# HGRN2, DeltaNet and S5 layer: three pieces of head 0's projections traced between S5's input groups

## The chip, the core and the metric

The kernel runs on one core of one Trainium2 chip. The metric is the device time of one execution in microseconds (us), the median over several executions.

The names of the engines: PE multiplies matrices, DVE, ACT and POOL work element by element (POOL the slowest, DVE and POOL on tensors, ACT with functions), and SP issues all DMAs here. Each engine takes its instructions from a row of its own, in the order of the row.

## What is computed

One layer of a backbone with three token mixers over 512 latent tokens and a prefix of 256 context tokens, of width 1024, in float32. After an RMSNorm and a modulation, one projection gives the inputs of all three: HGRN2 (four heads, both directions), a gated DeltaNet (four heads) and S5, a complex diagonal state space over 32 groups of 16 channels with 64 states. The three are mixed by gates; a residual add and an MLP follow. Of the reference, what this case touches is the preparation of HGRN2 and the scan of S5:

```python
qh = _heads(silu(q), A_HEADS);  vh = _heads(i, A_HEADS)
fval = lbb + (1.0 - lbb) * sigmoid(z)          # z: a forget gate per direction
args = [(qh, _heads(1.0 - fval[d], A_HEADS), vh, _heads(log(fval[d]), A_HEADS)) for d in range(2)]
...
def _s5_scan(u, ar, ai, bbr, bbi, x0r, x0i):
    """x_n = Lbar x_{n-1} + Bbar u_n from x0. u (B,N,G,16); returns state re/im (B,N,G,S)."""
```

The modulation comes from a product of the conditioning vector with a matrix `ada_w` of 1024 columns for each of its parts.

## The kernel before

The kernel is one program without loops on the chip: Python writes out every instruction, and a list scheduler then orders each engine's row. It goes by the order in which the instructions were traced, and pulls an instruction ahead where those before it in the trace must wait. All DMAs are issued by SP (L62), so they stand in one row too. Tiles come from pools, and a tile can be written only when the one that had its place is no longer read: `s4` (512 KB) has 8 places, `s2` 12, `nt` (1 MB) 2, `raw` 3, `hi` and `lo` 2 each, and in PSUM `pj` has 3, `tr` and `mm` 2 each, `att` 1.

`project` makes one block of 128 columns of the projection. Its weights are loaded (`raw`, 512 KB, L62), split into a rounded part on ACT (`hi`, L224) and the rest on DVE (`lo`, L225), and multiplied in three products (L245 to L247): 24 matmuls of 128x512 for the latent tokens, and 24 of 128x256 for the context where it is wanted.

The stretch in question follows the norm of the input. Its parts:

- S5's input u: four blocks of the projection (`U_C`, L1248 to L1254), each stored by two DMAs into `s5du` and `s5dul`.
- `state_in` (L347 to L374) makes S5's inputs, in eight groups of four channel groups. Each multiplies B by powers of the poles (`spread`, L337 to L346; groups 0, 1, 4, 5 and 6 on POOL, 2, 3 and 7 on DVE), transposes the result on PE (L364), copies it on ACT (L366), multiplies it by U on PE (L369; U is loaded for each second group) and copies that into `sv` (L371 to L373). Then `scan` (L376 to L385) steps through 94 tokens on POOL.
- `ada_gates` (L1228) sums three products of `ada_w` with the conditioning vector: 12 loads of 1 MB into `nt`, for each two sums on DVE (L1200; the first of each product on ACT, L1198), then sums over partitions on PE (L1211) and a small addition on DVE (L1212). One step of it is traced with each group of `state_in`, the last part (`last_sums`) later.
- `hgrn2_in` (L1264 to L1295) makes one head's inputs in five pieces: two gates F (`project`, tanh on ACT L1272, scaling on DVE L1273), the values V (with transposes on PE, L1282), then Q and G (ACT L1244, DVE L1245).
- `taps` (L417 to L447) makes S5's output filter, in eight groups as well: S5's C is loaded into an `nt` place, DVE prepares it (L425, two copies L431 and L432 for every second group) and multiplies it by powers of the poles (L408 to L410), PE transposes (L438 to L441), ACT copies (L443), and two DMAs store it (`s5dk`). Its DVE work is held behind what was traced for DVE before it (`queued`).
- Head 0's chunks then begin with cumulative sums on DVE (L514 to L518), transposes (L523), an ACT copy (L525), and products (L530, L552).

`mix` takes one piece of each of its generators in turn. Before, `hgrn2_in(0)`, `taps` and `last_sums` are mixed after all of S5's inputs.

Of the kernel before, what the change touches and what calls it, by code (L numbers as in the profile page):

```python
# [1031 lines left out]
def hybrid_block(ctx, tc, x, cc, xc, ada_w, columns, w_in, a_log, dt_bias, lam, s5_b, s5_c, w_glu, w_ba, w_bb, w_bc,  # L1032
# [18 lines left out]
    s5 = S5(k)  # L1051
# [113 lines left out]
    def project(col, lat=True, con=True, m=128, first=False):  # L1165

        wh, wl = W.load(w_in, col, 8, m)
        res = []
        for on, n, xh, xl in ((lat, 512, hh, hl), (con, 256, ch, cl)):
            if not on:  # L1170
                continue
            p = k.p("pj", [m, n])
            if first:
                for kt in range(8):
                    nc.tensor.matmul(p, wh[:, kt], xh[:, kt], start=kt == 0, stop=False)
                    nc.tensor.matmul(p, wl[:, kt], xh[:, kt], start=False, stop=False)
                for kt in range(8):
                    nc.tensor.matmul(p, wh[:, kt], xl[:, kt], start=False, stop=kt == 7)
            else:
                for kt in range(8):  # L1180
                    mm3(nc, p, wh[:, kt], wl[:, kt], xh[:, kt], xl[:, kt], kt == 0, kt == 7)
            res.append(p)
        return res if len(res) > 1 else res[0]
# [4 lines left out]
    def ada_rest(j, acc, fetch, engine):  # L1188

        kt = 0  # L1190
        while kt < 8:
            two = fetch()
            n = two.shape[1]
            k.dma(two, ada_w[128 * kt:128 * (kt + n), 1024 * j:1024 * j + 1024].rearrange("(x p) m -> p x m", p=128))
            for i in range(n):
                w, c = two[:, i], cs[:, kt + i, 0:1]
                if not kt + i:
                    nc.scalar.activation(acc, w, AF.Copy, scale=c)  # L1198
                elif engine is v:
                    v.scalar_tensor_tensor(acc, w, c, acc, op0=OP.mult, op1=OP.add)  # L1200
                else:
                    nc.scalar.activation(w, w, AF.Copy, scale=c)
                    engine.tensor_tensor(acc, acc, w, op=OP.add)
            kt += n
            if kt % 2 == 0:
                yield
        yield
        m = mod2[:, j - 2]
        p = k.p("att", [128, 8])
        for b in range(8):  # L1210
            nc.tensor.matmul(p[:, b:b + 1], acc[:, 128 * b:128 * b + 128], k.one, start=True, stop=True)  # L1211
        v.tensor_tensor(m, p, at["ada_b"][:, 8 * j:8 * j + 8], op=OP.add)  # L1212
        if j == 4:
            v.scalar_tensor_tensor(m, m, 1.0, at["n2"], op0=OP.add, op1=OP.mult)
            v.tensor_scalar(m, m, -1.0 / 256, None, op0=OP.mult)
        if j in (2, 5):
            if j == 2:
                v.tensor_scalar(m, m, 0.5, None, op0=OP.mult)
            p = k.p("att", [8, 128])
            nc.tensor.transpose(p, m, k.ident)  # L1220
            r = consts.tile([8, 128], FT, name=f"r{j}")
            nc.scalar.activation(r, p, AF.Copy)
            k.dma(drow[j // 3].rearrange("(b n) -> b n", b=8), r)
        yield

    def ada_gates():

        done = iter(())  # L1228
        for j in (2, 3, 4):
            g = ada_rest(j, k.t("s4", [128, 1024]), lambda: k.t("nt", [128, 2, 1024]), v)  # L1230
            for i in range(4):
                next(g)

                if i == 1:
                    for _ in done:
                        pass
                yield
            done = g
        yield done

    def silu2(out, p, x=None):

        t = k.t("pst", [128, p.shape[-1]])
        nc.scalar.activation(t, p, AF.Tanh, scale=0.5)  # L1244
        v.scalar_tensor_tensor(out, t, 1.0, p, op0=OP.add, op1=OP.mult)  # L1245


    for b in range(4):  # L1248
# [3 lines left out]
        nc.scalar.activation(u[:, :, 0:32], pc.rearrange("p (w r) -> p r w", r=8), AF.Copy)  # L1252
        k.dma(s5.du[b].rearrange("c g x -> g c x"), u.rearrange("p a b -> p (a b)"))
        k.dma(s5.dul[128 * b:128 * b + 128].rearrange("p (r w) -> p r w", r=8), u[:, :, 32:96])  # L1254
    ada = ada_gates()
    for _ in s5.state_in():
        next(ada)
    s5.scan()
    for last_sums in ada:
        pass  # L1260


    dn = {n: [k.d(f"n{n}{h}", [128, 512]) for h in range(4)] for n in "abc"}

    def hgrn2_in(h):

        F, FC = k.t("s4", [128, 2, 512]), k.t("s2", [128, 2, 256])
        for d in range(2):
            pl, pc = project(F_A + 512 * (1 - d) + 128 * h)
            z = 4 * d + h  # L1270
            for o, p in ((F[:, d], pl), (FC[:, d], pc)):
                nc.scalar.activation(o, p, AF.Tanh, scale=0.5)  # L1272
                v.tensor_scalar(o, o, lb[:, 1, z:z + 1], lb[:, 2, z:z + 1], op0=OP.mult, op1=OP.add)  # L1273
            yield
        V = k.t("s4", [128, 6, 128])
        pl, pc = project(V_A + 128 * h)
        for p, n, c0 in ((pc, 2, 0), (pl, 4, 2)):
            y = k.t("pst", [128, n, 128])
            nc.scalar.activation(y.rearrange("p a b -> p (a b)"), p, AF.Copy)
            pt = k.p("tr", [128, n, 128])  # L1280
            for t in range(n):
                nc.tensor.transpose(pt[:, t], y[:, t], k.ident)  # L1282
            nc.scalar.activation(V[:, c0:c0 + n], pt, AF.Copy)
        yield
        q = k.t("s2", [128, 512])
        silu2(q, project(Q_A + 128 * h, con=False))
        yield
        g = k.t("s2", [128, 512])
        silu2(g, project(G_A + 128 * h, con=False))
        heads[h] = HG(k, q, F, FC, V), g  # L1290
        yield
# [93 lines left out]
    def gate(n, b, to=None):  # L1385
        g = k.t("fg", [128, 512])
        nc.scalar.activation(g, project(GATES + 1024 * n + 128 * b, con=False), AF.Tanh, scale=0.5)
        if to is None:
            k.dma(dg[n][b], g)
        return g  # L1390

    def gates(n, blocks):
        for b in blocks:
            gate(n, b)
            yield
# [57 lines left out]
    def mix(*gs):  # L1453

        gs = list(gs)
        while gs:
            for g in list(gs):
                try:
                    yield next(g)
                except StopIteration:  # L1460
                    gs.remove(g)
# [12 lines left out]

    save = lambda to: lambda b, g: k.dma(to[b], g)
    s4 = lambda: k.t("s4", [128, 1024])
    taps = s5.taps()
    for _ in chain(mix(hgrn2_in(0), taps, last_sums), gates(0, range(0, 1))):
        pass
    weave(hgrn2(0), chain(hgrn2_in(1), context(0), gates(0, range(1, 2))), (3, 1), (4, 2), (1, 2), (8, 0), (2, 1))  # L1480
    weave(hgrn2(1), chain(hgrn2_in(2), mix(context(1), scalars_in())), (2, 1), (4, 1), (1, 1), (3, 2), (8, 3))
# [44 lines left out]
    for b, _ in enumerate(branch("b", w_bb, range(8), prev=mg[1], last=merged)):  # L1526
        wo += resident(w_out, 128 * b, 1, lambda shape: k.t("xn", shape), nc.gpsimd)
        if b >= 4:
            i = b - 4
# [297 lines left out]
```

## Time and profile before

| | |
|---|---|
| median of three executions | 1385.56 us (1382.54 to 1385.8) |
| profiled execution | 1387.55 us |
| its span, first to last instruction | 1385.8 us |
| mean granted clock of PE | 0.956 |
| PE busy | 1268.2 us (92%) |
| DVE, ACT, POOL busy | 957.0 (69%), 481.4 (35%), 338.7 us (24%) |
| DMA | 167.59 MB, 54.4% of 16 engines' time |

Busy times are of one execution. The granted clock is a share of 2.4 GHz, and at any moment it is 1 or 0.5. A row of the timeline has the start of an instruction, its time, the engine, the line of the kernel, the operation with its result and operands, and in brackets how long the engine had been idle before it and what ended that. Matmuls overlap, so the distance of two starts counts, not the time of one. In the table by stage the columns behind the stretch and its length are the busy times of PE, of PE's weight loads, of DVE, ACT and POOL (in brackets the number of instructions), then PE's granted clock, the mean share of the 16 DMA engines and the rate. The trace writes `s` for tiles of several pools and `in_s_c` for S5's C.

### The profile page before, as it was taken

Reading aid. Unit: us, or ns where it says so; the run is one execution under the profiler, and the core shown is the slowest. Engines: PE = TensorE matmul, PEld = TensorE weight load, DVE = VectorE, ACT = ScalarE, POOL = GpSimd, SP = SyncE. Lnnn points to the kernel's source line nnn. Section 1 sums busy time; section 2 is a strip of 40 time slices with the busy share of each in tenths; the row PEclk is TensorE's granted clock in tenths of the full one; section 3 lists DMA queues with packets and bytes.
Section 4 is the critical chain, followed back from the end, with each engine's and each line's share of the span. In section 5 each row is a group of like instructions: output and inputs, shape, how many; then the busy total and the mean of one; then the engine's idle time right before and its main releaser. Section 6 shows DMA issues by size and latency. Waiting matters only on the chain.

```text
span 1385.8 us, 18357 instructions
## 1 busy us (share of the span) xinstructions
PE 1268.2 (92%) x6781; PEld 1039.0 (75%) x6781; DVE 957.0 (69%) x1794; ACT 481.4 (35%) x889; POOL 338.7 (24%) x483
## 2 busy tenths in 40 slices
PE   7888899999999878899988899969979999999996
PEld 2477767888778777689876888847878878788885
DVE  6937677895777946988756975546657699674336
ACT  3425322433333435532233022233344345434222
POOL 0337599999400860000000000023000000000002
PEclk9889899999999989999998899979989999999998
DMA  9776752455856667581374345688405455633231
GB/s 360 139 129 213 180 74 42 62 107 43 82 78 114 87 86 192 111 94 23 72 123 151 84 87 108 133 194 268 123 16 182 137 154 155 178 95 103 91 107 61
DMA packets 184378, 167.59 MB, mean 121 GB/s; under 512 B 24865, under 2 KB 152545, under 8 KB 184289
## 3 DMA queue, kind: packets, MB, share of 16 engines
q1 hardware_dynamic: 184288, 166.43, 54.4%
q8 instruction: 53, 0.87, 0.3%
q14 instruction: 37, 0.30, 0.1%
HBM read 147.53 MB, written 18.87 MB: 120 GB/s over the span
## 4 chain that ended last, share of the span: by engine, by line
PE 63%; DVE 17%; DMA 13%; issue 4%; ACT 3%; SPq 1%; POOL 0%; POOLq 0%; DVEq 0%; ACTq 0%
PE pj L245 13%; PE pj L247 13%; PE pj L246 13%; DVE lo L225 3%; PE mm L887 3%; PE mm L878 2%; PE att L552 2%; DMA nt<-in_ada_w 2%; PE pj L1622 2%; DMA raw<-in_w_in 2%; DVE s L1200 1%; DMA xn<-in_w_out 1%; DMA s<-s5du 1%; DMA fg<-na 1%; PE mm L1622 1%
## 5 line engine op out<-in xcount | busy, mean ns | idle before, releaser
L225 DVE TENSOR_TENSOR lo<-raw,hi 128x1024 fp32r<-128x1024 f32 (+1 forms) x171 | 201.4, 1182 | 162.5 <-ACT hi L224 159.3
L224 ACT ACTIVATE hi<-raw 128x1024 fp32r<-128x1024 f32 (+1 forms) x171 | 164.6, 964 | 384.1 <-PE pj L246 241.9
L245 PE MATMUL pj<-hh,hi 128*128 128x512 f32 (+1 forms) x512 | 211.7, 413 | 4.9 <-ACT hi L224 4.5
L246 PE MATMUL pj<-hl,hi 128*128 128x512 f32 (+1 forms) x512 | 208.8, 408 | 0.0
L247 PE MATMUL pj<-hh,lo 128*128 128x512 f32 (+1 forms) x512 | 208.4, 407 | 0.0
L246 PE MATMUL pj<-hc,hi 128*128 128x512 f32 (+1 forms) x528 | 187.5, 355 | 0.0
L247 PE MATMUL pj<-h,lo 128*128 128x512 f32 (+1 forms) x304 | 116.9, 385 | 2.6 <-DVE lo L225 2.6
L245 PE MATMUL pj<-h,hi 128*128 128x512 f32 (+1 forms) x304 | 116.8, 385 | 2.5 <-ACT h L237 1.6
L245 PEld LDWEIGHTS pj<-hh,hi 128*128 128x128 f32 (+1 forms) x512 | 99.3, 194 | 23.9 <-ACT hi L224 5.0
L247 PEld LDWEIGHTS pj<-hh,lo 128*128 128x128 f32 (+1 forms) x512 | 98.5, 192 | 19.8 <-DVE lo L225 0.6
L246 PEld LDWEIGHTS pj<-hc,hi 128*128 128x128 f32 x528 | 102.7, 195 | 12.8 <-DVE hc L238 0.2
L246 PEld LDWEIGHTS pj<-hl,hi 128*128 128x128 f32 (+1 forms) x512 | 98.5, 192 | 17.3 <-issue 0.2
L245 PE MATMUL pj<-hc,hi 128*128 128x256 f32 (+2 forms) x256 | 84.9, 332 | 19.0 <-ACT hi L224 10.0
L247 PE MATMUL pj<-hc,lo 128*128 128x256 f32 (+2 forms) x256 | 84.5, 330 | 4.4 <-DVE lo L225 4.4
L1004 POOL TENSOR_SCALAR_AFFINE_SELECT s<-s 128x512 f32<-128x512 f32 x8 | 5.8, 753 | 301.3 <-DVE s L832 89.5
L1770 POOL TENSOR_TENSOR xn<-x,row 128x512 f32<-128x512 f32 x8 | 10.3, 1282 | 276.4 <-DVE x L1543 273.8
L247 PEld LDWEIGHTS pj<-h,lo 128*128 128x128 f32 x304 | 58.6, 193 | 14.5 <-DVE lo L225 3.8
L245 PEld LDWEIGHTS pj<-h,hi 128*128 128x128 f32 x304 | 58.7, 194 | 14.2 <-ACT h L237 2.0
L245 PEld LDWEIGHTS pj<-hc,hi 128*128 128x128 f32 (+1 forms) x256 | 50.6, 198 | 23.4 <-ACT hi L224 11.3
L247 PEld LDWEIGHTS pj<-hc,lo 128*128 128x128 f32 (+1 forms) x256 | 50.6, 197 | 8.5 <-DVE lo L225 5.9
L382 POOL TENSOR_TENSOR sw<-sp,sv 128x64 f32<-128x64 f32 x94 | 50.3, 535 | 20.6 <-ACT sv L372 13.4
L383 POOL TENSOR_TENSOR sw<-sp,sv 128x64 f32<-128x64 f32 x94 | 53.9, 574 | 0.0
(618 smaller groups left out, 2750.1 us busy)
## 6 DMA issues: line engine op xcount, KB each, us to landing
raw<-in_w_in SPq DMA_DIRECT2D x72, 512.0 KB
raw<-in_w_ff SPq DMA_DIRECT2D x66, 512.0 KB
nt<-in_ada_w SPq DMA_DIRECT2D x12, 1024.0 KB
aw<-in_ada_w SPq DMA_DIRECT2D x8, 512.0 KB
dg<-fg SPq DMA_DIRECT2D x16, 256.0 KB
fg<-dg SPq DMA_DIRECT2D x16, 256.0 KB
mg<-fg SPq DMA_DIRECT2D x16, 256.0 KB
fg<-mg SPq DMA_DIRECT2D x16, 256.0 KB
```

Of the source, the lines that this page charges most:

```text
L224: K.nc.scalar.activation(hi, w, AF.Copy)
L225: (engine or K.nc.vector).tensor_tensor(lo, w, hi.bitcast(FT), op=OP.subtract)
L245: nc.tensor.matmul(out, wh, xh, start=start, stop=False)
L246: nc.tensor.matmul(out, wh, xl, start=False, stop=False)
L247: nc.tensor.matmul(out, wl, xh, start=False, stop=stop)
L382: e.tensor_tensor(t[:, 1], aa[:, 1], ap(x, 96 * G, [[-96 * G, 2], [96, G]]), op=OP.mult)
L383: e.tensor_tensor(t[:, 0], aa[:, 0], x, op=OP.mult)
L552: nc.tensor.matmul(pa[:, c], kd[:, 128 * c:128 * c + 128], rhs, start=True, stop=True)
L878: nc.tensor.matmul(pq[:, u], M[:, u], ap(X, 128 * u, [[2 * m, 64 // m], [n + m, 2], [1, m]]), start=True, stop=True)
L887: nc.tensor.matmul(py[:, u], zt[:, u], q[:, u], start=True, stop=True)
L1200: v.scalar_tensor_tensor(acc, w, c, acc, op0=OP.mult, op1=OP.add)
L1622: nc.tensor.matmul(p[i], a[l][:, j, 128 * i:128 * i + 128], x[:, c], start=first and x is wh and not l, stop=last and x is wl)
```

## The change

The block that traces `ada_gates`, `state_in` and `scan` moves down, behind the definitions that `hgrn2_in` needs, and three pieces of `hgrn2_in(0)` are now drawn inside of it: both F after groups 1 and 3 and V after group 5. Q and G stay with the taps.

```diff
-    ada = ada_gates()
-    for _ in s5.state_in():
-        next(ada)
-    s5.scan()
-    for last_sums in ada:
-        pass
...
     s4 = lambda: k.t("s4", [128, 1024])
+    ada, into = ada_gates(), hgrn2_in(0)
+    for i, _ in enumerate(s5.state_in()):
+        next(ada)
+        if i in (1, 3, 5):
+            next(into, None)
+    s5.scan()
+    for last_sums in ada:
+        pass
+
     taps = s5.taps()
-    for _ in chain(mix(hgrn2_in(0), taps, last_sums), gates(0, range(0, 1))):
+    for _ in chain(mix(into, taps, last_sums), gates(0, range(0, 1))):
         pass
```

The lines of `hgrn2_in` are lower by 7 after the change (L1272 and L1273 become L1265 and L1266). The instructions are the same ones; the rows of PE, DVE, ACT, POOL and SP differ from S5's inputs to the end of the taps, and read alike again from L530 on.

SP at the last stores of u and the first ada loads, before (`nt` are ada loads, `raw` weights of the projection, `s<-s5du` U):

```order
L62 DMA raw_1987<-in_w_in 128x8x128
L62 DMA s_92_827<-s5du_561 128x8x96
L62 DMA s5dul<-s_90_820 1024x1x64
L62 DMA s_112_914<-s5du_562 128x8x96
L62 DMA s5du_564<-s_90_820 8x16x768
L62 DMA nt_954<-in_ada_w 128x2x1024
L62 DMA nt_996<-in_ada_w 128x2x1024
```

and after:

```order
L62 DMA raw_1936<-in_w_in 128x8x128
L62 DMA s_92_883<-s5du_561 128x8x96
L62 DMA s5dul<-s_90_820 1024x1x64
L62 DMA nt_1072<-in_ada_w 128x2x1024
L62 DMA s5du_564<-s_90_820 8x16x768
L62 DMA nt_1114<-in_ada_w 128x2x1024
L62 DMA nt_1219<-in_ada_w 128x2x1024
L62 DMA s_118_1032<-s5du_562 128x8x96
```

An ada load took the place of the second U, which stands behind three of them now.

SP up to the load of C (`nt<-in_s_c`), before:

```order
L62 DMA nt_1143<-in_ada_w 128x2x1024
L62 DMA nt_1185<-in_ada_w 128x2x1024
L62 DMA raw_2029<-in_w_in 128x8x128
L62 DMA raw_2259<-in_w_in 128x8x128
L62 DMA nt_1660<-in_ada_w 128x2x1024
L62 DMA nt_1664<-in_ada_w 128x2x1024
L62 DMA nt_1678<-in_ada_w 128x2x1024
L62 DMA nt_1682<-in_ada_w 128x2x1024
L62 DMA raw_2315<-in_w_in 128x8x128
L62 DMA nt_1804<-in_s_c 128x1024
```

and after:

```order
L62 DMA raw_2315<-in_w_in 128x8x128
L62 DMA drow<-r_1278 8x128
L62 DMA nt_1909<-in_ada_w 128x2x1024
L62 DMA nt_1913<-in_ada_w 128x2x1024
L62 DMA s_172_1352<-s5du_564 128x8x96
L62 DMA raw_2402<-in_w_in 128x8x128
L62 DMA nt_1927<-in_ada_w 128x2x1024
L62 DMA nt_1931<-in_ada_w 128x2x1024
L62 DMA raw_2487<-in_w_in 128x8x128
L62 DMA nt_1970<-in_s_c 128x1024
```

The two `raw` that stood together ahead of the last four ada loads are further up, and others stand singly between these loads.

DVE from C's first operation (L425) on, before:

```order
L425 TENSOR_SCALAR nt_1804<-nt_1804 128x512
L408 TENSOR_TENSOR nt_1805<-nt_1804,sp_422 128x512
L409 TENSOR_TENSOR s_284_1875<-nt_1804,sp_422 128x512
L408 TENSOR_TENSOR nt_1805<-nt_1804,sp_422 128x512
L410 TENSOR_TENSOR nt_1805<-nt_1805,s_284_1875 128x512
L1212 TENSOR_TENSOR mod_579<-att_1882,cols 128x8
L409 TENSOR_TENSOR s_284_1875<-nt_1804,sp_422 128x512
L1214 SCALAR_TENSOR_TENSOR mod_579<-mod_579,cols 128x8
L225 TENSOR_TENSOR lo_2262<-raw_2259,hi_2261 128x1024
```

and after:

```order
L425 TENSOR_SCALAR nt_1970<-nt_1970 128x512
L1212 TENSOR_TENSOR mod_579<-att_2023,cols 128x8
L225 TENSOR_TENSOR lo_2318<-raw_2315,hi_2317 128x1024
L1245 SCALAR_TENSOR_TENSOR s_298_1979<-pst_2011,pj_1986 128x512
L431 COPY nt_1970<-sp_422 64x16x16
L432 COPY nt_1970<-sp_422 64x16x16
L408 TENSOR_TENSOR nt_1971<-nt_1970,sp_422 128x512
L409 TENSOR_TENSOR s_303_2016<-nt_1970,sp_422 128x512
L408 TENSOR_TENSOR nt_1971<-nt_1970,sp_422 128x512
L410 TENSOR_TENSOR nt_1971<-nt_1971,s_303_2016 128x512
```

L1212, an L225, an L1245 and the copies L431 and L432 (which stood ahead of L425) are now between L425 and the first tap operations, L408 to L410.

## Rows read from the trace of the kernel before

**Rows 1.** Stages: us, each engine's busy us, granted clock, DMA share, GB/s.

```profile
92.80:175.00 82.20, 67.39 (x412) 58.42 (x411) 56.54 (x54) 35.71 (x80) 49.13 (x51) 0.88 0.70 186
175.00:240.70 65.70, 64.36 (x434) 45.78 (x433) 52.36 (x75) 13.31 (x20) 61.62 (x106) 0.99 0.40 57
240.70:352.00 111.30, 108.91 (x696) 93.93 (x696) 81.35 (x144) 41.53 (x77) 102.76 (x219) 1.00 0.54 72
174.99:233.65 58.66, 57.74 (x391) 41.23 (x391) 48.77 (x70) 12.10 (x17) 55.21 (x91) 0.99 0.39 54
178.58:240.30 61.72, 61.27 (x423) 43.66 (x423) 48.78 (x69) 11.37 (x17) 57.80 (x100) 1.00 0.39 57
```

**Rows 2.** PE's waits from 92 to 242 us: total, times, longest.

```profile
PE mm L369 <- DMA s<-s5du: 5.9, 1, 5.9
PE tr L364 <- POOL s L346: 3.6, 2, 2.8
PE mm L369 <- ACT s L366: 1.6, 2, 0.8
```

**Rows 3.** Table by stage, two shorter stretches.

```profile
137.00:146.00 9.00, 6.14 (x29) 5.60 (x30) 7.84 (x7) 2.34 (x6) 3.53 (x3) 0.62 1.04 212
151.66:155.60 3.94, 3.94 (x21) 3.94 (x22) 0.41 (x1) 1.25 (x4) 1.40 (x5) 0.58 0.38 148
```

**Rows 4.** Chain that ended last, in order of time: start, us, what.

```profile
97.87 1.14 SPq L62
...
101.22 8.73 DMA nt<-in_ada_w
...
139.60 16.19 DMA nt<-in_ada_w
...
166.25 8.71 DMA nt<-in_s_c
...
240.08 0.61 ACT s L525
...
353.17 13.77 DMA raw<-in_w_in
```

**Rows 5.** Timeline of DVE: start, us, operation, idle before and its releaser.

```profile
174.99 0.43 DVE L425 TENSOR_SCALAR nt<-nt 128x512 f32<-128x512 f32 x1 [3.05 <-DMA nt<-in_s_c]
...
233.65 0.85 DVE L514 TENSOR_TENSOR_SCAN s<-s,one 128x256 f32<-128x256 f32 x1
...
236.00 0.57 DVE L518 TENSOR_TENSOR s<-s,s 128x255 f32<-128x255 f32 x1
```

**Rows 6.** Timeline of PE.

```profile
176.99 0.39 PE L246 MATMUL pj<-hl,hi 128*128 128x512 f32 x1
177.22 0.40 PE L247 MATMUL pj<-hh,lo 128*128 128x512 f32 x1
...
178.58 0.39 PE L438 MATMUL tr<-nt,nt 128*48 128x128 f32 x2 [0.50 <-DVE mod L1212]
...
240.73 1.16 PE L530 MATMUL mm<-s,s 128*128 128x128 f32 x8 [0.45 <-ACT s L525]
```

**Rows 7.** DVE's groups from 174.9 to 233.7: busy us, mean ns, idle before.

```profile
L408 DVE TENSOR_TENSOR nt<-nt,sp 128x512 f32<-128x512 f32 x16 | 12.7, 824 | 0.0
...
L225 DVE TENSOR_TENSOR lo<-raw,hi 128x1024 fp32r<-128x1024 f32 x5 | 6.4, 1281 | 3.5 <-ACT hi L224 3.5
...
L1245 DVE SCALAR_TENSOR_TENSOR s<-pst,pj 128x512 f32<-128x512 f32 x2 | 1.4, 676 | 0.0
...
L431 DVE COPY nt<-sp 64x256 f32<-64x256 f32 x3 | 0.9, 291 | 4.7 <-PE tr L441 4.7
...
L1212 DVE TENSOR_TENSOR mod<-att,cols 128x8 f32<-128x8 f32 x1 | 0.2, 154 | 0.0
```

**Rows 8.** Timeline of POOL.

```profile
154.05 0.35 POOL L382 TENSOR_TENSOR sw<-sp,sv 128x64 f32<-128x64 f32 x1 [13.36 <-ACT sv L372]
...
451.28 1.50 POOL L456 TENSOR_SCALAR sp<-sp 128x512 f32<-128x512 f32 x1 [88.20 <-DMA sp<-in_s_c]
```


## Prediction

> **What bounds the kernel now.** I read the table of stages first [rows 1]. From 92.8 us (S5's first transposes) to 175 (the taps begin) PE works only 67.39 of 82.2 us, at a mean granted clock of 0.88; from 175 on it is full: 64.36 of 65.7, then 108.91 of 111.3. So time can be won where it waits or runs at its lower clock, and that is in the first of these stages. Their waits (82.2 - 67.39, and 65.7 - 64.36) are 16.15 us. The list of PE's waits [rows 2] says for what: 5.9 for the load of the first U, most of the rest for POOL's spreads and for ACT's copies of S5's transposes. The windows around 140 and 153 [rows 3] show the other loss: behind such waits PE's clock falls to 1.2 GHz, and its mean is 0.62 and 0.58 there.
>
> PE does not set the beginning of the taps, though. That is done by a chain through SP and DVE: loads of ada weights, with legs of 8.73 and 16.19 us, DVE's sums on them, and then the load of S5's C with 8.71 us [rows 4], after which DVE's first tap work, L425, starts at 174.99 [rows 5]. From the first tap transpose at 178.58 [rows 6] PE is the late one: there DVE idles 4.7 us for PE's transposes (L431) and 3.5 us for ACT's `hi` (L225) [rows 7].
>
> **The change part by part.** No operation is added or removed; some are moved.
>
> *Projections that go ahead of the taps.* By the printed order, PE has 101 matmuls of 128x512 and 72 of 128x256 between S5's first transposes and the first tap transpose before, and 147 and 72 now: 46 of 128x512 leave the taps stage. Two of them start 0.23 us apart at full clock [rows 6], so 46 x 0.23 = 10.6 us of PE work. The stage from the first L438 to the last matmul ahead of L530 holds 61.27 us of PE work now [rows 1], then 50.7.
>
> *Where they go.* Into PE's waits between 108 and 178. The 5.9 us for U stand ahead of all moved work and stay; of the 16.15 at most 10.3 can be filled, which is the limit of the gain at an unchanged clock. The fill should also keep the clock up where it fell: 6.14 x (1 - 0.62) + 3.94 x (1 - 0.58) = 4.0 us [rows 3].
>
> *When the taps can begin.* DVE's ada sums stay as they are. In SP's new order an ada load stands ahead of U1's load and S5's last store, at the place that SP reaches at 97.87 instead of 101.22 [rows 4]: 3.3 us early. Against it, DVE's row now mixes these sums with an L225 and an L1266 that wait for the moved projection, and has group 2's spread behind four more sums than before. I take L425 at 173.8, 1.2 us earlier. Bounds: 171.6 (all of the 3.3 kept) and 188.8 (the third rival). Behind L425 stand now, ahead of the four operations that make the first tap tile (0.8 us each), one L225 (1.28), one L1245 (0.68), two copies (0.3 each) and an addition of 0.2 (L1212) [rows 7]: with L425's 0.43, 6.4 us, so the first L438 is at 180.2, 1.6 us later than before.
>
> *The end of the stage.* By PE: 180.2 + 50.7 = 230.9, and L530 0.4 behind, as from 240.30 to 240.73 now [rows 1, 6]: 231.3. By DVE: from L425 to L514 it took 58.66 us [rows 5]; out of it go the 4.7 of waits for PE and 2.0 for an L225 and an L1245 that fall away behind L438, and 0.7 for two copies comes in: 52.7, so L514 at 226.5. Four more small DVE operations follow to 236.57 now [rows 5], 2.9 us; then four L523 and ACT's L525, which I estimate at 1.5 us together from the 0.61 of L525 [rows 4] and four transposes: L530 at 230.9. The two chains end within half a microsecond of each other and hand tiles to each other eight times; a wait of PE for ACT in S5's groups, the nearest such hand-over, is 0.8 us (1.6 in 2) [rows 2]. None would make it 231.3, one at each group 237.7; I take two or three, 2 us, since the transposes of a group have projections between them on PE. L530 moves from 240.73 to 233.2: **7.5 us**.
>
> *What is delayed.* S5's inputs. Until the last L369 PE now has 57 more matmuls of 128x512 and 48 more of half that: 57 x 0.23 + 48 x 0.12 = 18.9 us, of which some 9 fall into its waits. And POOL's row brings a spread of group 5 second, which needs a slot that group 2's transposes free, so POOL stands from about 110 to 124. The scan then starts near 164 instead of 154.05 [rows 8]. It costs nothing: behind the scan POOL waits 88.2 us for a load [rows 8], and nobody waits for the scan. Without that cover the price would be the 10 us.
>
> *Behind L530* every engine's order is the same in both, and PE is full to 352 [rows 1], so what is won is carried on. The next place that could swallow it is the weight load at 353.17, 13.77 us on the chain [rows 4]. It is issued when a buffer is free, behind the projections of that stage, so I let it move with them.
>
> The profiled execution took 1387.55 us (span 1385.8 and 1.75 around it), 2 above the median of 1385.56. Its sum is 1387.55 - 7.5 = 1380.05; from the median it is 1385.56 - 7.5 = **1378.0**.
>
> **Rivals.** *(1) More is won.* L425 stands at 171.6, L438 at 178, PE ends at 228.7 and nothing has to be handed over late: L530 at 229.1, 11.6 us, 1374. For it: SP's 3.3 us. Against: in the rest of its chain DVE has more ahead of it than before.
>
> *(2) No difference that can be told.* C is not earlier and DVE keeps its pace to L514: 174.99 + 58.66 + 4.4 = 238.05 for L530, 2.7 won, 1382.9. For it: DVE is busy for 48.77 of these 58.66 us [rows 1], and its 3.5 us for `hi` are not touched. A measurement of this kernel can tell no change under about 0.3% (4.2 us). The clock leads to the same: up to 175, where PE works in short bursts, its mean is 0.88 against 0.99 in the taps stage [rows 1]. If the taps become such a stage, 50.7 us take 50.7/0.88 = 57.6, L530 is at 238.2, 2.5 won, 1383.1. Against: PE has work for 51 of 53 us there. The Trainium skill, TensorE: Matmul & The Clock Gate, section "HAM oscillation — how this bites in real kernels", says that a kernel whose bursts of matmuls are parted by waits for data begins every burst at the low clock, and so speaks against thinning out the projections between the taps. At the two places of [rows 3] the trace agrees. *That it doesn't do what it says* belongs here too: the scheduler had pulled 101 matmuls ahead before; but 46 more are moved, so this could only make the gain smaller.
>
> *(3) Slower: weights overtake the ada loads.* SP's row now has single `raw` loads, 512 KB each, between the pairs of ada loads and ahead of C, where before two stood together and one ahead of C. The leg from 139.60, behind those two, took 16.19 us, the others 8.73 and 8.71 [rows 4]. One more leg of 16.2 puts L425 at 181.3 and L530 where it was: from there on it is a loss. Two put L425 at 188.8 and L530 at 248.2: 7.5 us lost, 1393. Against: the DMA engines' share is 0.70 in the mean up to 175 [rows 1], the bytes are the same, and loads that are spread out don't meet in one leg.
>
> **How the numbers follow.** The forecast, gains of 4.2 to 10: 0.45. (1), more than that: 0.12. (2), within 4.2 either way: 0.27. (3): 0.16. So faster 0.57, same 0.27, slower 0.16. The range reaches to 1390, short of the far half of (3), and to 1370, past the 1374 of (1) by the 4.0 us of the clock, which may come together with it: some 0.12 is left out.
>
> **What would show it.** Right: L425 between 173 and 175 and the first L438 near 180, L530 near 233, DVE busy for more than 0.85 of the taps stage with PE now waiting for its `nt`, a clock of 1.00 between 137 and 155, the scan some 10 us later with nobody waiting for it. Wrong: ada legs of 16 us in more than one place and L425 behind 181; a clock below 0.95 in the taps stage; or a time from L530 to the end that differs from now by more than 2 us.

## The result, and the profile after

The change makes the kernel slower: 1389.28 us against 1382.47 us, the medians of 20 executions each; the ratio is 1.0053 with a 95% interval of 1.0036 to 1.0071. (The kernel before had 1385.56 in the three executions shown ahead of the prediction; 1382.47 stands on more of them.) The profiled execution took 1390.33 us, its span is 1388.6. The trace of before is of an execution of 1387.55 us, slower than all 20 of this comparison (the slowest took 1386.01), so that traces and medians differ by some us.

In the two traces all of it lies where the change is. From the first L369, which waits for the first U in both, to L530 it took 140.06 us before (100.67 to 240.73) and 146.03 after (97.89 to 243.92): 6.0 us more. From L530 to the end of the span it was 1145.1 and 1144.7 (1137.8 to 1147.4 in the traces of the experiments). In the texts below every time "behind U" counts from that first L369, since the two traces differ by 2.8 us ahead of it.

The table by stage of the changed kernel (columns as in [rows 1]): U to the first tap transpose, from there to L530, the stretch from the ninth ada load to the load of C, and one around the last ada sum.

```profile
97.89:189.88 91.99, 78.87 (x454) 68.15 (x455) 58.73 (x64) 37.30 (x81) 48.18 (x54) 0.88 0.71 170
189.88:243.92 54.04, 50.42 (x378) 35.42 (x377) 43.20 (x61) 9.33 (x16) 50.67 (x88) 1.00 0.27 44
140.98:175.22 34.24, 29.23 (x179) 24.05 (x177) 17.57 (x17) 17.05 (x36) 11.79 (x16) 1.00 0.85 179
178.00:187.00 9.00, 8.55 (x28) 7.49 (x29) 5.72 (x10) 0.00 (x0) 8.29 (x19) 0.50 0.27 36
```

And of the kernel before, U to the first tap transpose, and the stretch from the ninth ada load to the load of C:

```profile
100.67:178.58 77.91, 68.48 (x408) 59.03 (x409) 52.32 (x50) 34.95 (x78) 52.55 (x56) 0.89 0.71 188
139.60:166.25 26.65, 23.54 (x137) 21.57 (x138) 15.00 (x16) 9.69 (x22) 12.67 (x19) 0.83 0.70 185
```

The second row is the gain: the tap stage has 50.42 us of PE work instead of the 61.27 of [rows 1] and takes 54.0 us instead of 62.15. The first row is the loss: the taps begin 92.0 us behind U, not 77.9. The third, beside the last row of before, shows what was going on there: the stretch takes 34.2 us, not 26.7, and the DMA engines' share is 0.85, not 0.70, at about the same rate (179 and 185 GB/s).

The chain that ended last, DMA legs among the ada loads (start, us):

```profile
115.69 11.93 DMA nt<-in_ada_w
...
140.98 14.36 DMA nt<-in_ada_w
...
157.94 13.87 DMA nt<-in_ada_w
```

In [rows 4] the chain had one long leg (16.19 us), one of 8.73 and C's of 8.71. SP's timeline (start, us, operation):

```profile
95.04 1.15 SPq L62 DMA_DIRECT2D nt<-in_ada_w  x1
...
109.79 3.08 SPq L62 DMA_DIRECT2D raw<-in_w_in  x1
...
119.22 1.73 SPq L62 DMA_DIRECT2D raw<-in_w_in  x1
133.57 0.37 SPq L62 DMA_DIRECT2D nt<-in_ada_w  x1
139.03 0.37 SPq L62 DMA_DIRECT2D raw<-in_w_in  x1
...
152.79 3.40 SPq L62 DMA_DIRECT2D raw<-in_w_in  x1
157.94 3.93 SPq L62 DMA_DIRECT2D nt<-in_ada_w  x2
165.06 0.37 SPq L62 DMA_DIRECT2D raw<-in_w_in  x1
175.22 0.35 SPq L62 DMA_DIRECT2D nt<-in_s_c  x1
```

Five weight loads are issued between U and C, where before there were three. C is issued 77.3 us behind U; before it was 65.6 (166.25 in [rows 4] less 100.67). What that does on DVE and PE:

```profile
178.81 0.43 DVE L425 TENSOR_SCALAR nt<-nt 128x512 f32<-128x512 f32 x1 [0.41 <-DMA nt<-in_s_c]
182.06 0.17 DVE L1212 TENSOR_TENSOR mod<-att,cols 128x8 f32<-128x8 f32 x1 [2.83 <-PE att L1211]
...
239.68 0.83 DVE L514 TENSOR_TENSOR_SCAN s<-s,one 128x256 f32<-128x256 f32 x1
```

```profile
178.45 3.57 PE L1211 MATMUL att<-one,s 128*128 128x1 f32 x16 [5.62 <-DVE s L1200]
...
183.31 0.63 PE L246 MATMUL pj<-hl,hi 128*128 128x512 f32 x1
183.74 0.63 PE L247 MATMUL pj<-hh,lo 128*128 128x512 f32 x1
...
189.88 0.42 PE L438 MATMUL tr<-nt,nt 128*48 128x128 f32 x2
```

PE has done by 172.8 what stands ahead of L1211 in its row, the sum of the last ada product, and waits 5.62 us for it. It comes out of this at half clock (0.50 from 178 to 187 in the table by stage): its 512-column matmuls then start 0.43 us apart, not 0.23 as in [rows 6], and some two dozen projections stand between L1211 and the first L438. On DVE, L1212 waits for that same sum and stands ahead of the taps. So L438 follows L425 by 11.1 us, not by the 3.6 of [rows 5, 6].

### The profile page after: what moved, and what is told of

Its sections match the earlier page's. It is cut to its first block, busy times and chain, and to the rows that moved or that the text cites. A ratio compares the mean times of both kernels' runs of the same rounds, so it can differ in the third digit from the quotient of the medians.

```text
span 1388.6 us, 18358 instructions
## 1 busy us (share of the span) xinstructions
PE 1265.6 (91%) x6781; PEld 1039.1 (75%) x6781; DVE 954.3 (69%) x1794; ACT 481.4 (35%) x889; POOL 335.7 (24%) x483
## 4 chain that ended last, share of the span: by engine, by line
PE 61%; DVE 17%; DMA 14%; issue 4%; ACT 3%; SPq 1%; POOL 0%; POOLq 0%; ACTq 0%; DVEq 0%
PE pj L245 12%; PE pj L247 12%; PE pj L246 12%; DVE lo L225 3%; DMA nt<-in_ada_w 3%; PE mm L887 2%; PE mm L878 2%; DMA s<-s5du 2%; PE att L552 2%; DMA xn<-in_w_out 2%; DMA raw<-in_w_in 2%; PE pj L1624 2%; PE pj L1122 1%; DVE s L1200 1%; DMA fg<-na 1%
## 5 line engine op out<-in xcount | busy, mean ns | idle before, releaser
L225 DVE TENSOR_TENSOR lo<-raw,hi 128x1024 fp32r<-128x1024 f32 (+1 forms) x171 | 200.6, 1177 | 158.3 <-ACT hi L224 150.9
L247 PEld LDWEIGHTS pj<-h,lo 128*128 128x128 f32 x304 | 58.6, 193 | 14.9 <-DVE lo L225 4.2
L382 POOL TENSOR_TENSOR sw<-sp,sv 128x64 f32<-128x64 f32 x94 | 47.4, 504 | 29.2 <-ACT sv L372 21.9
L385 POOL TENSOR_TENSOR sv<-sw 128x64 f32<-128x64 f32 x94 | 52.3, 557 | 7.4
```

Source lines behind the costliest of these rows:

```text
L225: (engine or K.nc.vector).tensor_tensor(lo, w, hi.bitcast(FT), op=OP.subtract)
L247: nc.tensor.matmul(out, wl, xh, start=False, stop=stop)
L382: e.tensor_tensor(t[:, 1], aa[:, 1], ap(x, 96 * G, [[-96 * G, 2], [96, G]]), op=OP.mult)
L385: e.tensor_tensor(y, t[:, 0], t[:, 1], op=OP.add)
```

## The experiments

Each was compared with the kernel before on the same chip. The table puts together what one trace of each shows, in us behind U, worked out from the starts in its timelines, and the ratio of its times to those of the kernel before.

```
                       C issued  L425   L438   L530   ratio (95%)
before                     65.6  74.3   77.9  140.1
after                      77.3  80.9   92.0  146.0   1.0053 (1.0036-1.0071)
e1  taps first             76.5  80.2   88.5  145.7   1.0049 (1.0032-1.0067)
e2  behind, taps first     66.4  74.7   81.0  140.6   1.0004 (0.9987-1.0020)
e3  first F behind 1       74.1  82.4   86.2  146.0   1.0042 (1.0027-1.0056)
e4  after, 4 KB rows       68.6  72.1   80.8  134.8   0.9943 (0.9923-0.9962)
e5  behind 3, 5, 7         80.4  84.0   91.9  146.5   1.0025 (1.0004-1.0046)
e6  first F behind 3       71.8  76.6   84.1  143.5   0.9990 (0.9976-1.0005)
e7  before, 4 KB rows      64.8  69.8   74.5  137.1   0.9955 (0.9936-0.9974)
e8  V alone                69.5  73.0   81.7  141.0   1.0004 (0.9987-1.0021)
e9  after, held            65.7  69.3   77.0  135.7   0.9975 (0.9956-0.9995)
e10 before, held           66.5  70.2   75.1  136.3   0.9997 (0.9975-1.0018)
e11 3, 5, 7, held, late    70.6  74.3   82.3  147.4   1.0064 (1.0038-1.0090)
e12 after, held, late      67.8  71.6   76.6  141.5   1.0016 (0.9997-1.0035)
e13 first F behind 1, held 73.0  76.6   81.6  141.4   1.0015 (1.0000-1.0031)
e14 3, 5, 7, held          73.0  76.7   85.4  148.7   1.0062 (1.0040-1.0084)
e15 first F behind 3, held 66.0  69.8   77.6  137.3   0.9975 (0.9961-0.9989)
```

One trace scatters by some us: e10 and the kernel before differ by nothing in their times, and by 3.8 us in the column of L530. The ratios decide; the columns say where. The trace of e6 is of its slowest execution, 1387.89 us.

### First: DVE's row, the place, or the loads

**e1** draws the taps ahead of head 0's pieces, so that the first tap tile follows L425 on DVE.

```diff
-    for _ in chain(mix(into, taps, last_sums), gates(0, range(0, 1))):
+    for _ in chain(mix(taps, into, last_sums), gates(0, range(0, 1))):
```

> The changed kernel, with the taps drawn ahead of head 0's pieces in each round, so that on DVE the first tap tile follows L425 at once and L1212 (which waits for PE's ada sums) stands behind it; SP's row up to the load of C is that of the changed kernel. Two theories. ROW: the loss comes from DVE's row between L425 and the first tap transpose, 11.1 us in the changed kernel against 3.6 before. Then L438 follows L425 by 4 to 5 us, L530 comes 5 to 7 us earlier than in the changed kernel (243.9), and the time is 1382 to 1384, no different from before. LOADS: the loss comes from the ada loads and C, which meet the weight loads. Then L425 stays at 178 to 179, the tap stage is held by what comes later, and the time is 1387 to 1390.

Measured: 1389.01 us. L438 came only 2.8 us nearer to L425, for PE still stood 4.88 us at L1211, and the time did not change. DVE's row behind C is not the cause by itself. What the theory on the loads said of this run (L425 unchanged, 1387 to 1390) came true.

**e2** draws the three pieces behind all of S5's inputs, with e1's order.

```diff
-        if i in (1, 3, 5):
-            next(into, None)
     s5.scan()
     for last_sums in ada:
         pass
+    for _ in range(3):
+        next(into)
```

> The three pieces are drawn behind S5's inputs, all three ahead of the taps, and the taps ahead of Q and G; SP's row up to C is that of the kernel before. LOADS: L425 is back at 175 within 1.5 us, against 178.8 in the changed kernel, and with the tap stage of 54 us the time is 1376 to 1380, faster than before. ROW alone: L425 makes no difference, and the time is the one of e1_taps_first.

Measured: 1381.56, the time of the kernel before. C is back (66.4), as expected; the gain that was expected with it is not there, for the stage from L425 to L530 takes 65.9 us, 65.7 before. Pieces that only change places with taps give nothing.

**e3** draws the first F alone, where the change has it.

```diff
-        if i in (1, 3, 5):
+        if i == 1:
```

> Only the first F piece is drawn between S5's inputs (behind group 1); the four others stay with the taps. On DVE L1212 stands behind the first tap tile as before. SP has the single weight loads between the ada loads as the changed kernel has. LOADS: L425 is at 178 or later, legs of the last ada loads over 11 us, and the time 1384 to 1388. ROW: L438 4 us behind L425, and the time 1380 to 1383.

Measured: 1385.88. One piece makes most of the loss, at L425 and not between L425 and L438 (3.8 us). That is what the loads would do, but also what a late ada sum would do.

**e4** reads the weights that are traced from S5's inputs to the end of head 0's chunks in long rows: 128 of 4 KB instead of 1024 of 512 bytes. It reads the same 512 KB each time, so it leaves the reference's weights out there, and the length of the rows and their one place are not told apart.

```diff
-        src = w[row:row + 128 * nk, col:col + m].rearrange("(k p) m -> p k m", p=128)
+        if self.wide and nk == 8 and m == 128:
+            src = w[0:128, 0:1024].rearrange("p (k m) -> p k m", k=8)
+        else:
+            src = w[row:row + 128 * nk, col:col + m].rearrange("(k p) m -> p k m", p=128)
```

> The changed kernel; the weights of the projection that are traced from S5's inputs to the end of head 0's chunks are read as 128 rows of 4 KB instead of 1024 rows of 512 bytes, the same 512 KB each (they are other weights, so what is computed from them isn't the reference's). LOADS: the weight loads hold the DMA engines for a shorter time, the last legs of ada loads (11.9, 14.4, 13.9 us) fall to 9 or less, L425 is 6 us or more earlier, and the time falls by 5 to 9 us from the changed kernel. ROW: the legs may fall, but L438 stays 8 us or more behind L425 and the time falls by 3 at most.

Measured: 1373.81, 15 us less than the changed kernel, where 5 to 9 were expected. With no instruction moved, C is 8.7 us earlier, and the table by stage shows the DMA engines at 0.66 where they had 0.85, from the ninth ada load to C:

```profile
135.22:164.56 29.34, 26.86 (x165) 23.54 (x164) 17.20 (x17) 15.12 (x32) 10.63 (x8) 0.92 0.66 204
```

**e7** is its control: the same long rows in the kernel before.

> The kernel before with the same weights read as 128 rows of 4 KB as in e4_weights_in_4k_rows (other weights, same bytes): the control of that run. If the small rows hurt only where weight loads meet ada loads (LOADS), this gains less than half of the 15 us that e4 gained, 1375 or more. If they hurt everywhere, it gains as much, 1364 to 1368, and e4 says nothing about the change.

Measured: 1376.13, so 6 us are gained in the order of before, 15 in the changed one. With cheap weight loads the changed kernel is no slower than the one before (0.9943 against 0.9955): the loss of the change is the price of its weight loads where they stand.

### Second: the place of the pieces

**e5**, **e6** and **e8** move the place: all three two groups later, the first F alone two groups later, V alone.

```diff
-        if i in (1, 3, 5):
+        if i in (3, 5, 7):
```

> All three pieces, drawn behind groups 3, 5 and 7 instead of 1, 3 and 5. On DVE the spreads of groups 2 and 3 stand where they stood before (ahead of the third ada tile), and L1212 behind the first tap tile; on SP single weight loads still stand between the ada loads. Two theories of the loss of 5.9 us between the first L369 and L530. SPREAD: the loss comes from DVE's row, where group 2's and 3's spreads stand behind L1266 and so move from 94 to 110 and into the time of the ada sums. Then L369 to L530 takes 140 us or less as before, and with the shorter taps 134 to 138; the time is 1374 to 1380. LOADS: it comes from the weight loads between the ada loads. Then the stretch is 144 to 147 as in the changed kernel, L425 is 80 us or more behind the first L369, and the time is 1386 to 1390.

```diff
-        if i in (1, 3, 5):
+        if i == 3:
```

> Only the first F piece, drawn behind group 3 instead of group 1: the one difference to e3_first_f_only is two groups of place. SPREAD: the loss of e3 goes, L369 to L530 140 us or less, time 1378 to 1382. LOADS: as e3, 146 us and 1385 to 1387.

```diff
-        if i in (1, 3, 5):
+        if i == 5:
```

> Only V, drawn behind group 5. DVE's early spreads are where they were, SP has a single weight load ahead of the last U and between the pairs of ada loads. SPREAD: no loss, and a part of the gain in the taps: 1376 to 1381. LOADS: some of the loss, L425 2 us or more later than before relative to the first L369, 1382 to 1386.

Measured: 1387.35, 1379.75 and 1382.22. e6 against e3 is the clearest: two groups of place are worth 0.5%. Behind group 1, the spreads of groups 2 and 3 (which DVE began at 94.36 in the kernel before, ahead of U) stand behind L1266, which waits for the F projection on PE, and they meet the ada sums later. But e5, where these spreads also stay in place, did not recover: C is at 80.4. So the spreads may be a part for a single piece, but are not the cause of the whole; the place changes other rows too, and no run moves the spreads alone.

### Third: which loads

None of the five weight loads ahead of C is of a moved piece: those are issued ahead of U in both kernels. A piece that is worked off early frees its `raw` places early, and the scheduler then pulls the loads of pieces to come (head 0's G, a gate, three of head 1) ahead, between the last ada loads and ahead of C, though PE needs the last of them only in the tap stage. Before, the first three of these five stood there. **e9** holds head 1's loads behind that of C; **e10** is the same hold in the kernel before. The hold is the one difference of e9 to the changed kernel in the source, but not in the rows: the scheduler then puts one ada sum further ahead on DVE, and behind C the first tap tile ahead of L1212 and 16 projections, not 23, between L1211 and L438. e1 has the tile in that place without the hold, and 17 projections, and gained nothing. (`behind_c` is set while head 1's pieces and what is mixed with them are written out, `c_load` is C's load.)

```diff
     def raw(self, src, shape):
         w = self.tile(shape)
-        self.K.dma(w, src)
+        if self.behind_c:
+            with self.K.tc.issue_after(self.K.c_load):
+                self.K.dma(w, src)
+        else:
+            self.K.dma(w, src)
         return w
```

> The changed kernel; only the weight loads of head 1's first pieces, which are needed in the tap stage but which SP issues between the last ada loads, are held behind the load of C. From the first L369 (U) to the issue of C it took 77.3 us in the changed kernel and 65.6 before, and to L530 146.0 and 140.1. PREFETCH: these early loads are what lengthens the legs of the last ada loads (14.4 and 13.9 us). Then C is issued 71 us or less behind the first L369, L530 comes 140 to 142 us behind it, and the time is 1380 to 1384. Otherwise (the loss lies in DVE's row or in U's late load) C stays at 75 or more and the time at 1386 or more.

> The same hold in the kernel before, as the control: there two weight loads stand together ahead of the last four ada loads and one ahead of C. PREFETCH: one or two of three are moved, C is 0 to 3 us earlier, and the time is 1378 to 1382. If it gains 5 us or more, the hold is good for any order and e9 says little about the change.

Measured: 1378.33 and 1381.83. With the hold the changed kernel has 11 us less than its 1389.28 and is faster than the one before by 0.25%; the control shows no change. SP's timeline of e9, and the stretch of the last ada loads in its table by stage:

```profile
109.80 3.07 SPq L62 DMA_DIRECT2D raw<-in_w_in  x1
...
119.55 1.63 SPq L62 DMA_DIRECT2D raw<-in_w_in  x1
...
155.16 3.48 SPq L62 DMA_DIRECT2D nt<-in_ada_w  x2
163.86 0.35 SPq L62 DMA_DIRECT2D nt<-in_s_c  x1
164.25 12.32 SPq L62 DMA_DIRECT2D raw<-in_w_in  x4
```

```profile
139.00:164.00 25.00, 24.33 (x162) 21.08 (x160) 17.64 (x18) 15.29 (x34) 8.66 (x6) 1.00 0.60 185
```

Two weight loads between U and C instead of five, a DMA share of 0.60, and from the eleventh ada load to C 8.7 us (155.16 to 163.86), where the changed kernel took 17.3 (157.94 to 175.22). C is issued 65.7 us behind U, as before the change. The stage from L438 keeps a part of its gain (58.6 us, 62.2 before), but from L425 on it takes 66.3 us, no less than before (65.7). What is earlier than before is L425: 3.7 us behind the issue of C, not 8.7 as in [rows 4, 5]. e10 has that too, and no gain in its times, so where e9's gain over the kernel before arises is not shown.

### Fourth: all undone, and what is left of the place

**e11** and **e12** add to the hold that L1211 and L1212 stand behind the first tap groups (with e1's order), with the pieces behind groups 3, 5 and 7, and behind 1, 3 and 5.

```diff
-        for b in range(8):
-            nc.tensor.matmul(p[:, b:b + 1], acc[:, 128 * b:128 * b + 128], k.one, start=True, stop=True)
-        v.tensor_tensor(m, p, at["ada_b"][:, 8 * j:8 * j + 8], op=OP.add)
+        with k.queued(*((nc.tensor, v) if j == 4 else ())):
+            for b in range(8):
+                nc.tensor.matmul(p[:, b:b + 1], acc[:, 128 * b:128 * b + 128], k.one, start=True, stop=True)
+            v.tensor_tensor(m, p, at["ada_b"][:, 8 * j:8 * j + 8], op=OP.add)
...
-    for _ in chain(mix(into, taps, last_sums), gates(0, range(0, 1))):
+    for _ in chain(mix(taps, into, late(last_sums, 4)), gates(0, range(0, 1))):
```

(`late` lets four rounds of the mix pass first.)

> All that was found undone at once, with all three pieces still between S5's inputs: drawn behind groups 3, 5 and 7 (DVE's early spreads stay), head 1's weights held behind C, the taps drawn ahead of head 0's Q and G, and the last ada sum on PE (L1211) and its addition on DVE (L1212) held behind the first tap groups. If these are the causes, L530 comes 133 to 137 us behind the first L369 (140.1 before, 146.0 after) and the time is 1374 to 1379, faster than before. If projections ahead of the taps are worth nothing, it is 139 to 141 and 1380 to 1383.

> As e11, but the pieces drawn behind groups 1, 3 and 5 as in the change: the difference to e11 is DVE's early spreads alone. SPREAD: 3 to 5 us slower than e11, L369 to L530 137 to 141. If the spreads don't matter once the loads are held: within 1.5 us of e11.

Measured: 1392.21 and 1384.54, misses both: if the spreads mattered, e11 was to be the faster by 3 to 5 us; it is the slower by 7.7. e12 is slower than e9 by 6 us: L438 is as early as in e9, but the stage from there takes 64.9 us instead of 58.6. So L1211's place ahead of the taps was no fault that this mends; e12 changes that place and the order of the taps together, and why it costs that much was not followed up.

**e13**, **e14** and **e15** are e3, e5 and e6 with the hold alone.

> e3_first_f_only (the first F behind group 1, 5 us slower than before) with head 1's weight loads held behind C. PREFETCH: the loss goes, 1378 to 1382. SPREAD: group 2's and 3's spreads still stand behind the ada sums on DVE, the second ada sum is still 55 us or more behind the first L369 (47.9 before, 57.2 in e3), and 3 us or more of the loss stay: 1384 to 1387.

> e5_two_groups_later (behind groups 3, 5 and 7) with the hold alone. SPREAD: better than e9 by 2 us or more, 1373 to 1376. PREFETCH alone: as e9, 1377 to 1380. If the late V piece (behind group 7) itself holds the ada sums on PE, as in e5 where the third was at 84 us, slower than e9: 1381 or more.

> e6_first_f_at_3 with the hold: the least change, one piece behind group 3. If the three pieces of the change are worth what e9 gained against e10 (3.5 us), one piece is worth 1 to 2: 1379 to 1381. If SPREAD matters more than the projections, it is as good as e9 or better: 1376 to 1378.

Measured: 1383.96, 1389.03 and 1377.5. The hold takes a good half of e3's loss (1.0042 to 1.0015). But e13 and e15, with the hold in both and one piece in each, still differ by 6.5 us: so the place has a price of its own, which the held loads don't explain. In e13's timeline DVE waits for the second ada sum in front of group 7's spread:

```profile
155.63 0.17 DVE L1219 TENSOR_TENSOR mod<-att,cols 128x8 f32<-128x8 f32 x1 [9.52 <-PE att L1218]
```

(L1218 and L1219 are L1211 and L1212 there.) That sum on PE, in e15, e9, e13 and e14 (their timelines):

```profile
147.16 1.84 PE L1218 MATMUL att<-one,s 128*128 128x1 f32 x16
148.80 1.84 PE L1218 MATMUL att<-one,s 128*128 128x1 f32 x16
153.75 1.84 PE L1218 MATMUL att<-one,s 128*128 128x1 f32 x16
157.49 1.84 PE L1218 MATMUL att<-one,s 128*128 128x1 f32 x16
```

It starts 48.4, 50.6, 56.1 and 58.9 us behind U (47.9 in the kernel before), and the times go with it: 1377.5, 1378.33, 1383.96 and 1389.03. No run moves this sum alone, so that it is the cause is not shown. e15 is as fast as e9 with one piece moved instead of three. e14 also shows a price of the hold where the pieces come late (e5 without it: 1.0025, e14: 1.0062): PE then waits for the held weights (its waits from 92 to 245 us: total, times, longest).

```profile
PE pj L251 <- ACT hi L230: 9.9, 2, 6.0
```

## Why the prediction was wrong

It forecast 1378.0 and faster; the kernel is slower, by what its third rival describes in kind. That the rival's price, 7.5 us, is near the 6.8 measured is luck: it put L425 88.1 us behind U, with 59.4 from there to L530; these were 80.9 and 65.1.

- *Fewer projections behind the first tap transpose*: right. PE's work in the stage fell by 10.9 us (forecast 10.6), and the stage from L438 to L530 took 54.0 us, forecast 53.0.
- *When the taps can begin*: this step failed. L425 was put at 173.8, 73.1 behind the U of that trace; it came at 80.9. I granted SP's ada load its 3.3 us, which it had (issued at 95.04, 2.85 ahead of U, where 101.22 was 0.55 behind it), and kept the later legs as they were. These were the ones that grew. The reason given against the third rival, that loads that are spread out don't meet in one leg, was the wrong one: the number of weight loads between U and C rose from three to five, and this could be read from the two pieces of SP's order in the section on the change (three in the second piece, two "further up"). e9, with three of them held, has no loss.
- *From L425 to L438*: forecast 6.4 us, measured 11.1. The 6.4 had DVE's own operations; it did not have PE, which was through with what stands ahead of L1211 and waited there for the last ada sum, with two dozen projections behind it in its row. Here the first mistake is paid a second time, at half clock. In e9, with the chain in time and 16 projections there, it was 7.7.
- *Where the projections go*: not into waits that vanish. PE's waits between U and L438 were 9.4 us (77.91 less 68.48 busy) and are 13.1 (91.99 less 78.87). The clock is 1.00 from 137 to 155, as forecast, but its mean is as low as before (0.88; 0.89 before): it fell at 130 to 140 (0.69) and 178 to 187 (0.50) instead. The rule of the Trainium skill on bursts parted by waits (TensorE: Matmul & The Clock Gate, "HAM oscillation — how this bites in real kernels") was weighed for the taps. The trace shows 1.00 there, and the burst that began slow stood ahead of them, behind the wait at L1211.
- *What is delayed*: right in kind. The scan starts 71.5 us behind U, forecast some 63, and nobody waits for it.
- *Behind L530*: right, 1144.7 against 1145.1 us.
- *The time from L425 on*: L425 to L530 is 62.4 to 68.0 us in both kernels and in e1 to e10, wherever the projections stand. When they leave the tap stage, the first L438 is later by nearly as much. The forecast had 59.4 (233.2 less 173.8).

With the loads held in both kernels, e9 against e10, the move is worth some 3.5 us in the medians, half of the 7.5 forecast, with intervals that overlap (0.9956 to 0.9995, 0.9975 to 1.0018). That it comes about as forecast is not shown: in their traces the stage from L438 is 2.5 us shorter in e9, but L438 is 1.9 later, and L530 only 0.6 earlier.

Open: what of the price of the place (e13 against e15, 6.5 us) is the displaced spreads, and why e9, with the first F behind group 1 too, does not pay it; and why e11 and e12, with the last ada sum behind the first tap groups, are so slow.

## What to carry to other kernels

Work that is moved earlier frees its buffers earlier, and so can bring forward the loads of the work behind it (here its own stood far ahead in both kernels); count all loads that then stand ahead of the transfer that a stage begins with. When a stage is made shorter, look at what its first operation waits for: here that was a chain of loads and sums, and moving matmuls could only lengthen it. A transfer that is needed late can be held behind one that is needed now; here that turned a loss of 0.5% into a gain of 0.25%. It is no rule: with the pieces two groups later the same hold gained nothing, and PE waited for what was held (e14).

## What the runs showed of the hardware

The share of the DMA engines' time says more than the rate. From the ninth ada load to C, 185 and 179 GB/s took 0.70 and 0.85 of it in the kernels before and after, and reading the weights in rows of 4 KB instead of 512 bytes, as many bytes from one place, brought it to 0.66 at 204 GB/s (e4) and gained 15 us. The Trainium skill, DMA: Bandwidth & Descriptors, section "Why small descriptors are slow (HBM only)", says that a fixed cost comes with each packet and each descriptor; the runs agree in the direction, and none of them measured the cost of one row.
